# Differential attention: both queries and both keys turned in one transpose each, sums of squares and norms behind the value product's emptying

## The chip, the cores and the metric

The kernel runs on one core of a Trainium2 chip. The metric is the device time of one execution in microseconds, the median of several runs. A core has a matrix engine (PE, TensorE, with its weight loads shown as PEld), three engines for vector work (DVE or VectorE, ACT or ScalarE, POOL or GpSimd), and a queue engine (SP, SyncE) that here issues most of the DMAs. Each engine runs its own instructions in order and waits for the others by semaphores.

## The reference

The program is one decoder layer for 1024 tokens of width 1024: three branches (an mLSTM, differential attention, cross-attention into a memory), gates, projections, and an MLP. The change lies in the differential attention: 8 heads, each with two queries and two keys of width 64 and a value of width 128.

```python
def diff_attention(q, k, v, q_g, k_g, lam, subln_g, lam_init):
    q = rms_norm(q, q_g)
    k = rms_norm(k, k_g)
    ...
        s = jnp.einsum('bhcqd,bhckd->bhcqk', qblk, kt).astype(jnp.float32) * scale
        ...
        s = jnp.where(kpos[None, :] <= qpos[:, None], s, -jnp.inf)
        p = jax.nn.softmax(s, axis=-1)
        a = p[:, :, 0] - lam * p[:, :, 1]
        return jnp.einsum('bhqk,bhkv->bhqv', a.astype(vt.dtype), vt)
    ...
    o = rms_norm(o, subln_g) * (1.0 - lam_init)
```

Here `c` counts the two queries and keys of a head, and `rms_norm` divides by the root of the mean square over the 64 (or 128) elements of a head.

## The kernel before

The branch stands at about 611 to 1156 us of the span. Products are kept near float32 by splitting an operand into a high part and a low part (the rest), and multiplying the parts.

**The projection** is `d_gemm` (L1036), a generator. One step, called a piece here, is three matmuls of 128 x 384 (`mm3`, one eighth of the 1024 inputs); `fill(n)` runs n pieces. Eight pieces make a tile of 128 tokens, with 384 columns: two queries, two keys (64 each) and a value (128). Four tiles make a half head, numbered j from 0 to 15, two to a head. Tiles alternate between two PSUM banks, `mm0` and `mm1`; `other_tile` gives the bank of the tile before, once that one is emptied, and the transposes called `pr` go there. At the end of a tile `evict` empties it: ACT casts the high part of the value (`dv`), DVE subtracts to get its low part, ACT copies queries and keys into `draw`, and ACT squares them into `dscr`. A closure put into `self.after` sums the squares on DVE into `drr`; with the fourth tile two POOL instructions (`rsqrt_mean`, L140 and L141, a power) make the reciprocal roots of the half head, and the list `self.prep` of the steps that turn queries and keys is set.

**The turns.** `draw` holds each query and each key twice over, side by side (the copy has a broadcast of 2). So one transpose of a 128 x 128 piece of it gives the 64 rows of a query on partitions 0 to 63 and again on 64 to 127; a turn is four such transposes, one for each tile. For a query, ACT casts the turn into `dq` with a factor, and DVE subtracts on one half of the partitions to get the low part there; the high part stays on the other. For a key, ACT copies the turn into `dk` (the high part, on both halves) and DVE subtracts into `dkl` (the low part, both halves). The keys are scaled by `drr` before their turns, by four DVE multiplications; the queries are scaled later, in the exponential. There are four turns in a half head: query 0, query 1, key 0, key 1.

**The main loop** of `branch_d` (L1112) has 64 slots and five more to drain, eight to a head, one for each tile of queries. Slots are numbered by their place in the head (0 to 7) below. A prologue of eight steps (L1254) runs the projection of the first two half heads. In slot s stand, in this order in the code: the scores of the first query (`scores(s, 0)`: matmuls `sc`, then on DVE a mask with a maximum, shown as CUSTOM_DVE_ANT_0, and a small step, then on ACT the exponential `dpe`), `after()`, the combination of the two softmaxes of slot s - 1 (`combine`: a reciprocal, a small step and the wide `dpe` on DVE), four pieces, the value product of slot s - 2 (`po`, emptied by ACT and DVE into `doS`), the first function of the list `prep`, a piece, the scores of the second query, the transposes `tp` of the combined softmax of slot s - 1 with their emptying into `daT`, the second exponential, the remaining pieces, and the second function of `prep`. The norm of the attention's output, per half head, is cut into parts 0 to 3 (`norm`): squares, a sum with the power on POOL, a multiplication of `doS`, and a turn `tp<-doS` whose emptying is `yd`. Weights (`w<-raw`) are cast and split in between, by `ahead`.

DVE and ACT are wrapped in `InOrder` here, so both run in the order of the code. The pools give the buffers: `tp` and `po` share a ring of two banks, `sc` has two.

The lines of `evict`, before, on which much hangs:

```python
            A.copy(rw, ps[:, 0:256].rearrange("p (a d) -> p a d", a=4).unsqueeze(2).broadcast_to([P, 4, 2, 64]))
            scr = pool.tile([P, 256], F32, tag="dscr", name=self.name("dscr"))
            A.activation(scr, ps[:, 0:256], AF.Square)
```

Of the kernel before, what the change touches and what calls it, by code (L numbers as in the profile page):

```python
# [10 lines left out]
F32 = mybir.dt.float32  # L11
F32R = mybir.dt.float32r
# [5 lines left out]
P = 128  # L18
# [13 lines left out]
def f32(ap):  # L32
    return ap.bitcast(F32)
# [38 lines left out]
class Layer:  # L72
# [963 lines left out]
    def d_gemm(self, pool, kv):  # L1036
# [40 lines left out]

        def evict(ps, i, raws, vh, rr):
            v = pool.tile([P, 2, P], F32R, tag="dv", name=self.name("dv"))
            self.split2(v[:, 0], v[:, 1], ps[:, 256:384])  # L1080
            rw = pool.tile([P, 4, 2, 64], F32, tag="draw", name=self.name("draw"))
            A.copy(rw, ps[:, 0:256].rearrange("p (a d) -> p a d", a=4).unsqueeze(2).broadcast_to([P, 4, 2, 64]))
            scr = pool.tile([P, 256], F32, tag="dscr", name=self.name("dscr"))
            A.activation(scr, ps[:, 0:256], AF.Square)
            raws.append(rw)
            vh.append(v)

            def rest():
                V.tensor_reduce(rr[:, i], scr.rearrange("p (a d) -> p a d", a=4), axis=AX.X, op=ALU.add)
                if i == 3:  # L1090
                    rl = rr.rearrange("p a b -> p (a b)")
                    self.rsqrt_mean(rl, rl, 64, 16)
                    self.prep = turns(raws, rr, vh)

            self.after.append(rest)

        for j in range(16):
# [3 lines left out]
            vh, raws = [], []  # L1101
            for i in range(4):
# [6 lines left out]
                evict(ps, i, raws, vh, rr)  # L1109
                yield True  # L1110

    def branch_d(self, pool, dw):  # L1112
# [140 lines left out]

        for n in range(8):  # L1254
            fill(1)
            after()
            fill(3)
            p = self.prep.pop(0) if self.prep else None
            if p:
                p[0]()  # L1260
            fill(2)
            ahead(n)
            fill(2)
            if p:
                p[1]()
        for s in range(NS + 5):
# [4 lines left out]
            after()  # L1271
            if 1 <= s <= NS:
                combine(s - 1)
            if hh >= 1 and i == 0:
                norm(hh - 1, 1)
            fill(4)
            if 2 <= s < NS + 2:
                values(s - 2)
            if hh >= 1 and i == 1:
                norm(hh - 1, 2)  # L1280
            p = self.prep.pop(0) if self.prep else None
            if p:
                p[0]()
            fill(1)
# [24 lines left out]
            fill(2)  # L1309
            if p:  # L1310
                p[1]()
# [506 lines left out]
    def run(self):  # L1818
        tc, nc = self.tc, self.nc
        with ExitStack() as ctx:  # L1820
# [22 lines left out]
            with ExitStack() as c1:  # L1843
# [33 lines left out]
                with self.rings(("rpg", 2), ("ptm", 1), ("wpg", 14)) as (self.rp, ptm, self.wp):  # L1877
# [7 lines left out]
                    with tc.tile_pool(name="pd", bufs=2) as pd, tc.tile_pool(name="pd3", bufs=3) as pd3, tc.tile_pool(name="pdm", bufs=1) as pdm, tc.tile_pool(name="pd5", bufs=7) as pd5, tc.tile_pool(name="pdv", bufs=5) as pdv, tc.tile_pool(name="pdv2", bufs=17) as pdv2, tc.tile_pool(name="pd4", bufs=4) as pd4:  # L1885
# [6 lines left out]
                        class T4:  # L1892
                            def tile(_, shape, dt, tag, name):
                                tag = "dscr2" if tag == "gt" else tag
                                p = pd5 if tag == "draw" else pdv if tag == "drr" else pdv2 if tag == "dv" else pd4 if tag in ("dk", "dkl") else pdm if tag == "dpe1" else pd3 if tag in ("daT", "dst") else pdm if tag in ("dscr", "dscr2", "y") else pd
                                return p.tile(shape, dt, tag=tag, name=name)
# [76 lines left out]
```

## Time and profile before

| | |
|---|---|
| median of 3 runs | 2192.08 us (2191.87 to 2197.32) |
| the profiled execution | 2194.59 us, of which the span is 2192.80 |
| granted clock of PE, mean | 0.999 |
| transposes `pr` | 256, in 64 turns |
| ACT's copies `draw`, 128x512 | 64, median 0.587 us |
| DVE's multiplications `draw`, 128x256 | 64, median 0.418 us |
| DVE's sums of squares `drr` | 64, mean 0.417 us |
| POOL's power on `drr` | 16, mean 2.90 us |

The span is the time from the first to the last instruction in the record; the execution takes 1.79 us more around it. Times within the span are given from its start. A row of the timeline has the start, the duration, the engine, the line, the operation, what it writes and reads, and the shapes; in brackets stands how long the engine sat idle before it, and who ended that. A helper at L67 records all of DVE's and ACT's instructions of the branch, so they are told apart by the names of what they write and read.

### The profile page before, as it was taken

The page shows a single profiled execution, that of the slowest core. Times are in us where ns is not written, and L with a number is a line of the kernel's source. Part 1 is how long each engine was busy: PE and PEld are TensorE (multiplying, and loading weights), DVE is VectorE, ACT ScalarE, POOL GpSimd, SP SyncE. Part 2 cuts the span into 40 slices and gives each one's busy share as a digit, 9 for nine tenths or more (in the row PEclk, how much of TensorE's full clock was granted, in tenths as well). Part 3 has the DMA queues.
Part 4 walks back from the last instruction along what each step waited for, and adds up shares of the span by engine and source line. Part 5 has one row for each costly group of instructions (what it writes and reads, how often), then busy time and mean ns, then how long its engine had stood idle before and what let it go on. Part 6 is the DMA issues. An engine that isn't in the chain of part 4 may idle for free.

```text
span 2192.8 us, 30563 instructions
## 1 busy us (share of the span) xinstructions
PE 2166.7 (99%) x11254; PEld 1874.8 (85%) x11254; DVE 1385.5 (63%) x2628; ACT 969.5 (44%) x1949; POOL 534.9 (24%) x709
## 2 busy tenths in 40 slices
PE   8999999999999999999999999999999999999998
PEld 6888789888899999999888888888878888788887
DVE  6455457554138888888753233454588778876678
ACT  7543445444246666666543111223433333543331
POOL 3210000000011111111100002101566667564444
PEclk9999999999999999999999999999999999999999
DMA  7032222201311111110135344435534454744442
GB/s 252 21 117 87 88 62 79 79 14 63 116 49 35 35 31 39 39 37 25 54 120 173 116 139 130 144 111 177 191 126 159 154 198 158 268 165 158 159 158 96
DMA packets 110947, 242.38 MB, mean 111 GB/s; under 512 B 10921, under 2 KB 19406, under 8 KB 108750
## 3 DMA queue, kind: packets, MB, share of 16 engines
q1 hardware_dynamic: 108494, 227.85, 31.4%
q10 hardware_dynamic: 2304, 12.58, 1.4%
q8 instruction: 88, 1.44, 0.3%
q14 instruction: 61, 0.50, 0.1%
HBM read 173.25 MB, written 67.14 MB: 110 GB/s over the span
## 4 chain that ended last, share of the span: by engine, by line
PE 77%; DVE 12%; ACT 4%; DMA 4%; issue 2%; POOL 1%; SPq 0%; ACTq 0%; POOLq 0%; DVEq 0%
PE mm L92 46%; PE p L92 21%; PE sc L92 4%; PE tp L95 2%; PE po L92 2%; DVE sc L67 1%; ACT dpe L67 1%; DVE dpe L67 1%; DMA raw<-in_wkv 1%; DVE wo L67 1%; DVE draw L67 1%; PE pr L95 1%; DVE dst L67 1%; DVE u L67 1%; POOL wraw L67 1%
## 5 line engine op out<-in xcount | busy, mean ns | idle before, releaser
L92 PE MATMUL mm<-hT,w 128*128 128x512 f32 x1920 | 464.2, 395 | 1.6 <-ACT gt L605 1.6
L92 PE MATMUL mm<-w,hT 128*128 128x384 f32 (+3 forms) x2496 | 454.6, 329 | 0.0
L92 PEld LDWEIGHTS mm<-hT,w 128*128 128x128 f32 x1920 | 353.5, 188 | 75.5 <-ACT gt L605 2.0
L92 PEld LDWEIGHTS mm<-w,hT 128*128 128x128 f32 x2496 | 388.2, 188 | 8.8
L67 POOL TENSOR_TENSOR wraw<-wraw 128x128 f32<-128x128 f32 x496 | 321.3, 672 | 171.3 <-DMA wraw<-in_wdown 127.6
L92 PE MATMUL p<-xo,wo 128*128 128x512 f32 x1344 | 307.6, 390 | 2.2 <-ACT u L67 0.7
L92 PE MATMUL p<-xd,wo 128*128 128x512 f32 x1344 | 305.7, 389 | 0.6 <-DVE acc L67 0.5
L92 PEld LDWEIGHTS p<-xo,wo 128*128 128x128 f32 x1344 | 251.3, 188 | 57.1 <-DVE u L67 2.3
L92 PEld LDWEIGHTS p<-xd,wo 128*128 128x128 f32 x1344 | 252.0, 188 | 54.1 <-DVE acc L67 1.0
L92 PE MATMUL mm<-kt,w 128*128 128x512 f32 x1152 | 261.3, 389 | 0.0
L92 PEld LDWEIGHTS mm<-kt,w 128*128 128x128 f32 x1152 | 216.3, 188 | 44.8
L67 ACT CAST wo<-wraw 128x896 fp32r<-128x896 f32 x125 | 116.5, 944 | 258.1 <-POOL wraw L67 119.7
L67 DVE TENSOR_TENSOR wo<-wraw,wo 128x896 fp32r<-128x896 f32 x125 | 155.7, 1254 | 111.6 <-ACT wo L67 109.6
L67 ACT ACTIVATE dpe<-sc,dst,drr 128x256 f32<-128x256 f32 (+7 forms) x128 | 106.7, 833 | 62.0 <-DVE dst L67 51.9
L116 ACT CAST w<-raw 128x256 fp32r<-128x256 f32 (+2 forms) x128 | 69.0, 567 | 126.6 <-PE mm L92 99.5
L117 DVE TENSOR_TENSOR w<-raw,w 128x256 fp32r<-128x256 f32 (+2 forms) x128 | 81.5, 664 | 41.7 <-ACT w L116 41.7
L67 DVE CUSTOM_DVE_ANT_0 sc<-sc,tmask 128x256 f32<-128x256 f32 (+7 forms) x128 | 96.9, 757 | 3.6 <-PE sc L92 2.4
L140 POOL TENSOR_SCALAR hss<-hss 128x4 f32<-128x4 f32 x8 | 3.5, 442 | 378.0 <-ACT mscr L907 378.0
L92 PE MATMUL mm<-mh,w 128*128 128x512 f32 x256 | 78.9, 389 | 0.0
L106 DVE TENSOR_TENSOR w<-raw,w 128x256 fp32r<-128x256 f32 (+1 forms) x64 | 27.1, 439 | 80.0 <-ACT w L105 79.4
L67 DVE TENSOR_TENSOR w<-raw,w 128x384 fp32r<-128x384 f32 (+2 forms) x112 | 65.8, 598 | 15.8 <-ACT w L67 15.6
L92 PEld LDWEIGHTS po<-dv,daT 128*128 128x128 f32 x576 | 74.8, 189 | 0.9
(325 smaller groups left out, 2947.2 us busy)
## 6 DMA issues: line engine op xcount, KB each, us to landing
wraw<-in_wup SPq DMA_DIRECT2D x64, 256.0 KB, 3.2
r_d<-xts SPq DMA_DIRECT2D x16, 1024.0 KB, 4.2
xd<-r_d SPq DMA_DIRECT2D x16, 1024.0 KB, 5.4
wraw<-in_wdown SPq DMA_DIRECT2D x64, 256.0 KB, 4.2
raw<-in_wgate SPq DMA_DIRECT2D x48, 256.0 KB, 3.1
gates<-gt SPq DMA_DIRECT2D x48, 256.0 KB, 2.1
raw<-in_wd SPq DMA_DIRECT2D x32, 384.0 KB, 3.1
kraw<-y SPq DMA_DIRECT2D x24, 512.0 KB, 4.6
```

Source lines behind the costliest of these rows:

```text
L67: return self.tc.keep_in_program_order(f(*a, **k))
L92: self.pin(self.nc.tensor.matmul(out, l, r, start=start, stop=stop))
L95: self.pin(self.nc.tensor.transpose(out, x, self.ident))
L106: low = lambda: self.V.tensor_sub(lo, src, f32(hi))
L116: nc.scalar.copy(hi, src)
L117: nc.vector.tensor_sub(lo, src, f32(hi))
L140: g.tensor_scalar(r, ss, 1.0 / width, EPS, op0=ALU.mult, op1=ALU.add)
```

## The change

`draw` is one buffer for the four tiles of a half head, and holds each query and key once. A turn transposes the two queries at once (query 0 comes to partitions 0 to 63, query 1 to 64 to 127), a second one the two keys: two turns per half head. ACT copies the two halves of the partitions by two instructions of 64 x 512, and DVE subtracts by two. The low part of a query is written to the other half of the partitions from the one it is read from. A key's high part is copied to the other half by a DMA from SBUF to SBUF (`twice`, two per half head); its low part is kept on its own half only, in four lasting buffers (`kls`) whose other halves are set to zero once. The scaling of the keys is one multiplication. The turns stand in the list as (nothing, query turn), (scaling, key turn), (nothing, the DMAs): the first function of an entry runs behind `combine`, the second behind the value product. The list is set at the end of the fourth tile, not with the last sum of squares. `after()` comes behind the second function, parts 1 and 2 of the norm at the end of the slot, and the pieces of a slot are cut into 4, 2, 1 and 1 (before 4, 1, 1 and 2). Two pools get other sizes.

```diff
--- before.py
+++ after.py
@@ -1039,50 +1039,59 @@
         nc = self.nc
         V, A = self.V, self.A
         self.after, self.prep = [], []
-
-        def turns(raws, rr, vh):
+        kls = [pool.tile([P, 2, 512], F32R, tag=f"dkl{i}", name=f"dkl{i}") for i in range(4)]
+        for t in kls:
+            nc.gpsimd.memset(f32(t[64:128, 0]), 0.0)
+            nc.gpsimd.memset(f32(t[0:64, 1]), 0.0)
+
+        def turns(rw, rr, vh, j):
 
             qT = pool.tile([P, 2, 512], F32R, tag="dq", name=self.name("dq"))
             kd = pool.tile([P, 2, 512], F32R, tag="dk", name=self.name("dk"))
-            kl = pool.tile([P, 2, 512], F32R, tag="dkl", name=self.name("dkl"))
+            kl = kls[j % 4]
+            own = (slice(0, 64), slice(64, 128))
 
             def turn(c):
                 pt = self.other_tile()
                 for i in range(4):
-                    self.transpose(pt[:, i * P : (i + 1) * P], raws[i][:, c].rearrange("p a d -> p (a d)"))
+                    self.transpose(pt[:, i * P : (i + 1) * P], rw[:, i, 2 * c : 2 * c + 2].rearrange("p a d -> p (a d)"))
                 return pt
 
-            def q_(c):
-                lo = slice(64 - c * 64, 128 - c * 64)
-                pt = turn(c)
-                A.activation(qT[:, c], pt, AF.Copy, scale=self.gd)
-                V.scalar_tensor_tensor(
-                    out=qT[lo, c], in0=pt[lo], scalar=self.gd[lo], in1=f32(qT[lo, c]), op0=ALU.mult, op1=ALU.subtract
-                )
+            def q_():
+                pt = turn(0)
+                for c in range(2):
+                    A.activation(qT[own[c], c], pt[own[c]], AF.Copy, scale=self.gd[own[c]])
+                for c in range(2):
+                    V.scalar_tensor_tensor(
+                        out=qT[own[1 - c], c], in0=pt[own[c]], scalar=self.gd[own[c]], in1=f32(qT[own[c], c]),
+                        op0=ALU.mult, op1=ALU.subtract,
+                    )
 
             def scale():
-                for i in range(4):
-                    k_ = raws[i][:, 2:4].rearrange("p c a d -> p c (a d)")
-                    V.tensor_mul(k_, k_, rr[:, i, 2:4].unsqueeze(2).broadcast_to([P, 2, P]))
-
-            def k_(c):
-                pt = turn(2 + c)
-                A.copy(kd[:, c], pt)
-                V.tensor_sub(kl[:, c], pt, f32(kd[:, c]))
-                if c == 1:
-                    kv.append((qT, kd, kl, vh, rr))
+                k_ = rw[:, :, 2:4]
+                V.tensor_mul(k_, k_, rr[:, :, 2:4].unsqueeze(3).broadcast_to([P, 4, 2, 64]))
+
+            def k_():
+                pt = turn(1)
+                for c in range(2):
+                    A.copy(kd[own[c], c], pt[own[c]])
+                for c in range(2):
+                    V.tensor_sub(kl[own[c], c], pt[own[c]], f32(kd[own[c], c]))
+
+            def twice():
+                for c in range(2):
+                    nc.sync.dma_start(f32(kd[own[1 - c], c]), f32(kd[own[c], c]))
+                kv.append((qT, kd, kl, vh, rr))
 
             none = lambda: None
-            return [(lambda: q_(0), none), (lambda: q_(1), scale), (lambda: k_(0), none), (lambda: k_(1), none)]
-
-        def evict(ps, i, raws, vh, rr):
+            return [(none, q_), (scale, k_), (none, twice)]
+
+        def evict(ps, i, rw, vh, rr, j):
             v = pool.tile([P, 2, P], F32R, tag="dv", name=self.name("dv"))
             self.split2(v[:, 0], v[:, 1], ps[:, 256:384])
-            rw = pool.tile([P, 4, 2, 64], F32, tag="draw", name=self.name("draw"))
-            A.copy(rw, ps[:, 0:256].rearrange("p (a d) -> p a d", a=4).unsqueeze(2).broadcast_to([P, 4, 2, 64]))
+            A.copy(rw[:, i], ps[:, 0:256].rearrange("p (a d) -> p a d", a=4))
             scr = pool.tile([P, 256], F32, tag="dscr", name=self.name("dscr"))
             A.activation(scr, ps[:, 0:256], AF.Square)
-            raws.append(rw)
             vh.append(v)
 
             def rest():
@@ -1090,15 +1099,17 @@
                 if i == 3:
                     rl = rr.rearrange("p a b -> p (a b)")
                     self.rsqrt_mean(rl, rl, 64, 16)
-                    self.prep = turns(raws, rr, vh)
 
             self.after.append(rest)
+            if i == 3:
+                self.prep = turns(rw, rr, vh, j)
 
         for j in range(16):
             hd, hf = divmod(j, 2)
             w = self.dw[hd]
             rr = pool.tile([P, 4, 4], F32, tag="drr", name=self.name("drr"))
-            vh, raws = [], []
+            rw = pool.tile([P, 4, 4, 64], F32, tag="draw", name=self.name("draw"))
+            vh = []
             for i in range(4):
                 s = slice((hf * 4 + i) * P, (hf * 4 + i + 1) * P)
                 ps = self.mm_tile(384)
@@ -1106,7 +1117,7 @@
                     self.mm3(ps, (self.hT[:, k, 0, s], self.hT[:, k, 1, s]), w[k], k == 0, k == NK - 1)
                     if k < NK - 1:
                         yield True
-                evict(ps, i, raws, vh, rr)
+                evict(ps, i, rw, vh, rr, j)
                 yield True
 
     def branch_d(self, pool, dw):
@@ -1251,37 +1262,36 @@
                 A.activation(y, pt, AF.Copy, scale=self.gsub)
                 self.store_y(1, hh // 2, hh % 2, y)
 
+        self.after, self.prep = [], []
         for n in range(8):
+            p = self.prep.pop(0) if self.prep else (None, None)
             fill(1)
+            if p[0]:
+                p[0]()
+            fill(1)
+            if p[1]:
+                p[1]()
             after()
-            fill(3)
-            p = self.prep.pop(0) if self.prep else None
-            if p:
-                p[0]()
-            fill(2)
+            fill(4)
             ahead(n)
             fill(2)
-            if p:
-                p[1]()
         for s in range(NS + 5):
             hh, i = divmod(s - 2, 4)
             more = s < NS
             if more:
                 scores(s, 0)()
-            after()
+            p = self.prep.pop(0) if self.prep else (None, None)
             if 1 <= s <= NS:
                 combine(s - 1)
-            if hh >= 1 and i == 0:
-                norm(hh - 1, 1)
-            fill(4)
+            if p[0]:
+                p[0]()
+            fill(4 if s > 1 else 2)
             if 2 <= s < NS + 2:
                 values(s - 2)
-            if hh >= 1 and i == 1:
-                norm(hh - 1, 2)
-            p = self.prep.pop(0) if self.prep else None
-            if p:
-                p[0]()
-            fill(1)
+            if p[1]:
+                p[1]()
+            after()
+            fill(2 if s > 1 else 4)
             if hh >= 1 and i == 2:
                 norm(hh - 1, 3)
             if more:
@@ -1306,9 +1316,9 @@
                     exp()
                 fill(1)
                 lows()
-            fill(2)
-            if p:
-                p[1]()
+            if hh >= 1 and i < 2:
+                norm(hh - 1, 1 + i)
+            fill(1)
             if 2 <= s < NS + 2 and i == 3:
                 norm(hh, 0)
         assert self.gdone == 288 and len(kv) == 16
```

What the code's order becomes on two engines, at three places. First DVE in slot 4 of the first head, from the last small steps of the first scores over the combination of slot 3 (`dpe`) to the mask of the second scores (the ISA row with `sc`; another ISA row reads its maximum). `dst` are the small steps of the softmax, and the row of `drr` with `dscr` is a sum of squares. Before:

```order
L67 ISA dst_6865 128x1
L67 SCALAR_TENSOR_TENSOR dst_6865<-dst_6865,drr_6391 128x1
L67 TENSOR_REDUCE drr_6592<-dscr_6861 128x4
L67 RECIPROCAL dst_6790<-dst_6790 128x2
L67 SCALAR_TENSOR_TENSOR dst_6790<-dst_6790,dv 128x1
L67 SCALAR_TENSOR_TENSOR dpe_6788<-dpe_6789,dst_6790,dpe_6788 128x512
L67 SCALAR_TENSOR_TENSOR doS_6742<-po_6897,dst_6715,doS_6742 128x128
L67 SCALAR_TENSOR_TENSOR dq_6877<-pr_6906,dv,dq_6877 64x512
L67 ISA sc_6916,dst_6865<-sc_6916,tmask 128x640
L67 ISA dst_6865 128x1
L67 SCALAR_TENSOR_TENSOR dst_6865<-dst_6865,drr_6391 128x1
```

Now:

```order
L67 SCALAR_TENSOR_TENSOR dst_6846<-dst_6846,drr_6402 128x1
L67 RECIPROCAL dst_6777<-dst_6777 128x2
L67 SCALAR_TENSOR_TENSOR dst_6777<-dst_6777,dv 128x1
L67 SCALAR_TENSOR_TENSOR dpe_6775<-dpe_6776,dst_6777,dpe_6775 128x512
L67 SCALAR_TENSOR_TENSOR doS_6734<-po_6873,dst_6708,doS_6734 128x128
L67 SCALAR_TENSOR_TENSOR dq_6842<-pr_6882,dv,dq_6842 64x512 x2
L67 TENSOR_REDUCE drr_6582<-dscr_6840 128x4
L67 ISA sc_6900,dst_6846<-sc_6900,tmask 128x640
L67 ISA dst_6846 128x1
L67 SCALAR_TENSOR_TENSOR dst_6846<-dst_6846,drr_6402 128x1
```

The sum of squares went from ahead of the reciprocal to behind the query turn's subtractions, of which there are now two, and so stands between them and the mask.

Second, DVE in slot 5 of the same head, from the first mask's small step to the second mask. Before:

```order
L67 SCALAR_TENSOR_TENSOR dst_6955<-dst_6955,drr_6391 128x1
L67 TENSOR_REDUCE drr_6883<-dscr_6951 128x4
L67 RECIPROCAL dst_6865<-dst_6865 128x2
L67 SCALAR_TENSOR_TENSOR dst_6865<-dst_6865,dv 128x1
L67 SCALAR_TENSOR_TENSOR dpe_6863<-dpe_6864,dst_6865,dpe_6863 128x640
L67 SCALAR_TENSOR_TENSOR doS_6742<-po_6981,dst_6790,doS_6742 128x128
L67 SCALAR_TENSOR_TENSOR dq_6877<-pr_6992,dv,dq_6877 64x512
L67 ISA sc_7002,dst_6955<-sc_7002,tmask 128x768
```

Now:

```order
L67 SCALAR_TENSOR_TENSOR dst_6935<-dst_6935,drr_6402 128x1
L67 RECIPROCAL dst_6846<-dst_6846 128x2
L67 SCALAR_TENSOR_TENSOR dst_6846<-dst_6846,dv 128x1
L67 SCALAR_TENSOR_TENSOR dpe_6844<-dpe_6845,dst_6846,dpe_6844 128x640
L67 TENSOR_TENSOR draw_6583<-draw_6583,drr_6582 128x4x128
L67 SCALAR_TENSOR_TENSOR doS_6734<-po_6961,dst_6777,doS_6734 128x128
L67 TENSOR_TENSOR dkl_6245<-pr_6972,dk_6843 64x512 x2
L67 TENSOR_REDUCE drr_6858<-dscr_6931 128x4
L67 ISA sc_6988,dst_6935<-sc_6988,tmask 128x768
```

The multiplication of `draw`, on which the key turn waits, now stands behind `dpe`; the two `dkl` of the key turn follow in the same slot. The subtraction of query 1 is gone from here, since it stands in slot 4.

Third, PE in the prologue, from the first piece of the fifth tile on: each `mm` row is a piece, `pr` rows are turns. Before:

```order
L92 MATMUL mm_6392<-w_6085,hT 128x384 x3
L92 MATMUL mm_6392<-w_6103,hT 128x384 x3
L92 MATMUL mm_6392<-w_6123,hT 128x384 x3
L92 MATMUL mm_6392<-w_6141,hT 128x384 x3
L95 MATMUL pr_6411<-ident,draw_6277 128x128
L95 MATMUL pr_6411<-ident,draw_6313 128x128
L95 MATMUL pr_6411<-ident,draw_6351 128x128
L95 MATMUL pr_6411<-ident,draw_6387 128x128
L92 MATMUL mm_6392<-w_6159,hT 128x384 x3
L92 MATMUL mm_6392<-w_6177,hT 128x384 x3
L92 MATMUL mm_6392<-w_6192,hT 128x384 x3
L92 MATMUL mm_6392<-w_6207,hT 128x384 x3
```

Now:

```order
L92 MATMUL mm_6404<-w_6085,hT 128x384 x3
L92 MATMUL mm_6404<-w_6103,hT 128x384 x3
L95 MATMUL pr_6411<-ident,draw_6256 128x128 x4
L92 MATMUL mm_6404<-w_6123,hT 128x384 x3
L92 MATMUL mm_6404<-w_6141,hT 128x384 x3
L92 MATMUL mm_6404<-w_6159,hT 128x384 x3
L92 MATMUL mm_6404<-w_6177,hT 128x384 x3
L92 MATMUL mm_6404<-w_6192,hT 128x384 x3
L92 MATMUL mm_6404<-w_6207,hT 128x384 x3
L92 MATMUL mm_6452<-w_6085,hT 128x384 x3
L92 MATMUL mm_6452<-w_6103,hT 128x384 x3
L95 MATMUL pr_6460<-ident,draw_6256 128x128 x4
```

The query turn comes after two pieces of a tile, not four, and its four transposes read one buffer. The key turn follows one tile later, where the turn of query 1 was before.

More of the change, by code (lines that the diff above doesn't have):

```diff
@@ L1884, in run @@
                                 next(dw)
-                    with tc.tile_pool(name="pd", bufs=2) as pd, tc.tile_pool(name="pd3", bufs=3) as pd3, tc.tile_pool(name="pdm", bufs=1) as pdm, tc.tile_pool(name="pd5", bufs=7) as pd5, tc.tile_pool(name="pdv", bufs=5) as pdv, tc.tile_pool(name="pdv2", bufs=17) as pdv2, tc.tile_pool(name="pd4", bufs=4) as pd4:
+                    with tc.tile_pool(name="pd", bufs=2) as pd, tc.tile_pool(name="pd3", bufs=3) as pd3, tc.tile_pool(name="pdm", bufs=1) as pdm, tc.tile_pool(name="pd5", bufs=2) as pd5, tc.tile_pool(name="pdv", bufs=5) as pdv, tc.tile_pool(name="pdv2", bufs=17) as pdv2, tc.tile_pool(name="pd4", bufs=4) as pd4:
                         self.tmask = ptm.tile([P, D], F32, name="tmask")
@@ L1894, in tile @@
                                 tag = "dscr2" if tag == "gt" else tag
-                                p = pd5 if tag == "draw" else pdv if tag == "drr" else pdv2 if tag == "dv" else pd4 if tag in ("dk", "dkl") else pdm if tag == "dpe1" else pd3 if tag in ("daT", "dst") else pdm if tag in ("dscr", "dscr2", "y") else pd
+                                p = pd5 if tag == "draw" else pdv if tag == "drr" else pdv2 if tag == "dv" else pd4 if tag == "dk" else pdm if tag.startswith("dkl") else pdm if tag == "dpe1" else pd3 if tag in ("daT", "dst") else pdm if tag in ("dscr", "dscr2", "y") else pd
                                 return p.tile(shape, dt, tag=tag, name=name)
```

## The prediction

> **What bounds the kernel now.** I read the page's head first, then the busy time by stretches, the waits of PE, and last the timeline of one head of the differential attention, where the change lies.
>
> ```profile
> span 2192.8 us, 30563 instructions
> PE 2166.7 (99%) x11254; PEld 1874.8 (85%) x11254; DVE 1385.5 (63%) x2628; ACT 969.5 (44%) x1949; POOL 534.9 (24%) x709
> 604.00:646.00 42.00, 42.00 (x239) 40.50 (x238) 13.04 (x30) 15.60 (x37) 3.11 (x2) 1.00 0.17 51
> 820.00:880.00 60.00, 59.53 (x394) 57.70 (x394) 51.49 (x138) 41.47 (x97) 8.61 (x8) 1.00 0.12 36
> ```
>
> The last two lines are stretches: width, then busy us of PE, PEld, DVE, ACT and POOL, the granted clock, the DMA share and GB/s. In the prologue of the stage (604 to 646) and in its steady part (820 to 880) PE is full at clock 1.00, and the DMA engines are nearly idle. So a matmul that goes shortens the stage, and a wait of PE lengthens it. In the steady part DVE too is busy 51.5 of 60 us: chains that run over DVE and end at PE are the danger.
>
> **What goes.** Each of the 16 half heads loses two of its four turns (a turn is four transposes `pr`): 32 turns, of which two stood in the prologue.
>
> ```profile
> 832.24 0.42 PEld L95 LDWEIGHTS pr<-ident,draw 128*128 128x128 f32 x4
> 832.63 0.47 PEld L92 LDWEIGHTS mm<-w,hT 128*128 128x128 f32 x3
> 630.38 0.53 PEld L95 LDWEIGHTS pr<-ident,draw 128*128 128x128 f32 x4
> 630.88 4.14 PEld L92 LDWEIGHTS mm<-w,hT 128*128 128x128 f32 x24
> ```
>
> The timeline (start, duration, engine, line, operation) shows a turn between two pieces of projection: from its first weight load to the next one's 0.39 us in a steady slot, 0.50 in the prologue. The saving is 30 x 0.39 + 2 x 0.50 = 12.7 us.
>
> Some waits of PE go as well, since DVE's queue is rearranged around them: the sums of squares leave the place ahead of the combination `dpe`, and four multiplications per half head become one.
>
> ```profile
> PEld tp L95 <- DVE dpe L67: 3.7, 7, 0.5
> PEld tp L95 <- DVE doS L67: 2.7, 7, 0.4
> PE tp L95 <- DVE doS L67: 2.3, 7, 0.8
> PE tp L95 <- DVE dpe L67: 1.5, 7, 0.2
> ```
>
> These are us in total, times, and the longest, in the stage. Once per head each, the transposes `tp` wait for DVE, in slot 0 (of a head's eight) for `doS` and in slot 2 for `dpe`. The weight loads lose 6.4 us, the matmuls 3.8; I take the middle, 5.1. In slot 0 the reduction of 0.4 us ahead of `dpe` goes and `tp` comes a piece of projection later; in slot 2 the four multiplications at the end of slot 1 go. The norm's steps, put off to the end of slots 2, 3, 6 and 7, take DVE time there instead, but slots 6 and 7 lose two subtractions `dkl` and slot 6 the four multiplications. Saved in all: **17.8 us**.
>
> ACT's copies `draw` are half as wide, which shortens nothing, as the steps behind them wait for DVE. The 32 new DMAs of 128 KB (`dk` to its own other half) are issued on SP behind ACT's copies and are needed two slots, some 10 us, later: nothing for PE, and 0.12 of the DMA engines in use leaves room. If that cover went, the first scores of a half head would wait. The eight memsets run on POOL before the stage, where it is idle.
>
> **What is new on the path.** The two halves of a turn are now emptied by a pair: ACT copies both, and only then DVE subtracts both, as DVE's first subtraction waits for ACT's second copy. The reduction of the sums stands behind the pair. The k turn stands one slot after the q turn, and its transposes wait for the scaling of k. So a chain now runs from PE, in slot 4, to PE in slot 5. Before, that scaling had two slots. The rows of that place, in one head:
>
> ```profile
> 851.03 0.42 PEld L95 LDWEIGHTS pr<-ident,draw 128*128 128x128 f32 x4
> 851.73 0.69 ACT L67 ACTIVATE dq<-pr,dv 128x512 fp32r<-128x512 f32 x1
> 852.45 0.76 DVE L67 SCALAR_TENSOR_TENSOR dq<-pr,dv,dq 64x512 fp32r<-64x512 f32 x1 [0.43 <-ACT dq L67]
> 853.35 0.83 DVE L67 CUSTOM_DVE_ANT_0 sc<-sc,tmask 128x640 f32<-128x640 f32 x1
> 853.81 0.59 ACT L67 CAST daT<-tp 128x512 fp32r<-128x512 f32 x1 [0.42 <-PE tp L95]
> 854.29 0.52 ACT L67 CAST w<-raw 128x384 fp32r<-128x384 f32 x1
> 854.70 0.89 ACT L67 ACTIVATE dpe<-sc,dst,drr 128x640 f32<-128x640 f32 x1
> 855.58 0.26 ACT L67 CAST dv<-mm 128x128 fp32r<-128x128 f32 x1
> 855.87 0.29 DVE L67 TENSOR_TENSOR dv<-mm,dv 128x128 fp32r<-128x128 f32 x1 [0.28 <-ACT dv L67]
> 856.08 0.96 DVE L67 CUSTOM_DVE_ANT_0 sc<-sc,tmask 128x768 f32<-128x768 f32 x1
> 857.13 0.16 DVE L67 SCALAR_TENSOR_TENSOR dst<-dst,drr 128x1 f32<-128x1 f32 x1
> 857.21 0.41 DVE L67 TENSOR_REDUCE drr<-dscr 128x4 f32<-128x256 f32 x1
> 857.53 0.15 DVE L67 RECIPROCAL dst<-dst 128x2 f32<-128x2 f32 x1
> 857.98 0.89 DVE L67 SCALAR_TENSOR_TENSOR dpe<-dpe,dst,dpe 128x640 f32<-128x640 f32 x1
> 858.77 0.42 PEld L95 LDWEIGHTS pr<-ident,draw 128*128 128x128 f32 x4
> 860.19 0.74 DVE L67 SCALAR_TENSOR_TENSOR dq<-pr,dv,dq 64x512 fp32r<-64x512 f32 x1 [0.42 <-ACT dq L67]
> 860.85 0.95 DVE L67 CUSTOM_DVE_ANT_0 sc<-sc,tmask 128x768 f32<-128x768 f32 x1
> 845.50 0.68 DVE L67 TENSOR_TENSOR doS<-doS,dso 128x512 f32<-128x512 f32 x1
> ```
>
> PE's way between the two turns is 858.77 - 851.03 = 7.74 us, with the same work after the change. The new chain, by steps from start to start: turn to first copy 0.70; to the second copy 0.58 (ACT starts the next 0.11 before a listed end, 853.81 to 854.29); to the first subtraction 0.72; two subtractions 0.66 each (860.19 to 860.85); the reduction 0.32 (857.21 to 857.53). Sum 3.64: the mask of the slot's second scores starts at 854.67, not 853.35. From there all is in line on two full queues: to ACT's exponential 1.35, behind it the cast `dv` 0.88, DVE's `dv` 0.29, the next mask 0.21, its small step 1.05, the reciprocal 0.08 (no reduction between), `dpe` 0.45, its own 0.80 (0.89 less what DVE overlaps), the scaling, and 0.03 to PE. The scaling is one multiplication of 128 x 512; the nearest row is the `doS` multiplication, 0.68. Sum 5.82. The chain takes 9.46 us, and PE waits 1.72; seven heads make **12.0 us**. (POOL's power is in time: it needs 3.3 us after the reduction, and the scaling stands 5 us behind.) Behind the waiting turn stands all of PE's slot, so nothing wins this back.
>
> The same chain runs from slot 0 to slot 1, with smaller scores:
>
> ```profile
> 823.63 0.42 PEld L95 LDWEIGHTS pr<-ident,draw 128*128 128x128 f32 x4
> 826.45 0.30 DVE L67 CUSTOM_DVE_ANT_0 sc<-sc,tmask 128x128 f32<-128x128 f32 x1
> 829.14 0.42 DVE L67 CUSTOM_DVE_ANT_0 sc<-sc,tmask 128x256 f32<-128x256 f32 x1
> 829.65 0.16 DVE L67 SCALAR_TENSOR_TENSOR dst<-dst,drr 128x1 f32<-128x1 f32 x1
> 830.94 0.35 DVE L67 SCALAR_TENSOR_TENSOR dpe<-dpe,dst,dpe 128x128 f32<-128x128 f32 x1
> ```
>
> The second mask starts at 823.63 + 3.64 = 827.27, which is 0.82 late; so the next at 829.96, its small step 0.51 later, then 0.08, 0.45, 0.27 for the narrow `dpe` (0.35 less 0.08), 0.68 and 0.03: 831.98. PE, without the old wait of about 0.4, is there at 832.24 - 0.4 = 831.83. It waits 0.15: 7 x 0.15 = **1.0 us**, more if the chain is longer, since the slack is used up.
>
> In the prologue PE does projection alone, and there the power on POOL is in the way:
>
> ```profile
> 630.20 0.42 DVE L67 TENSOR_REDUCE drr<-dscr 128x4 f32<-128x256 f32 x1 [0.94 <-ACT dscr L67]
> 631.06 2.90 POOL L141 TENSOR_TENSOR drr<-drr,mhalf 128x16 f32<-128x16 f32 x1
> 635.01 0.53 PEld L95 LDWEIGHTS pr<-ident,draw 128*128 128x128 f32 x4
> ```
>
> A piece of projection is (635.01 - 630.88) / 8 = 0.52 us. The q turn now comes after two pieces, not four, at 629.35, and waits until the tile is emptied, about 630.0 (the reduction behind the emptying began at 630.20, and ACT's copy is now half as wide; with 630.2 it would be 0.2 more): 0.65. From 630.0 the reduction begins 3.32 later; from a reduction's start to the end of the power it is 633.96 - 630.20 = 3.76; the scaling 0.71: 637.8. PE is at the k turn at 630.0 + 0.5 + 8 x 0.52 = 634.6: a wait of 3.2. The second half head has the scores between, some 0.5: 2.7, and about 0.6 at its q turn. Sum **7.1 us**.
>
> **The sum.** -17.8 + 12.0 + 1.0 + 7.1 = +2.3 us. The profiled execution took 2194.59 (span 2192.80 and 1.79 around it) and would become 2196.9; the median of the runs shown is 2192.08, so the forecast is **2194.4**. A measurement of this kernel tells about 0.3%, 6.6 us, from no change: no change, by gains and new waits that cancel.
>
> **The rivals.**
> First, the pair runs side by side. Before, a subtraction started 0.03 us after the end of the copy it reads (852.45 behind 851.73 + 0.69), and if the first did so again, each of the 16 chains would be 0.58 shorter: 7 x 0.58 + 1.0 + 2 x 0.58 = 6.3 us, giving 2188. Against it: both halves lie in one bank, and the program puts the wait on the second copy. [...] No row of before shows two engines at once in one `pr`. Chance 0.10.
>
> Second, faster: the waits in slots 5 and 1 don't come, because a link of the chain is looser than the rows (the exponential or the cast that follows it). Then only the prologue's 7.1 stand against 17.8: 2181. For it: DVE gets lighter in every other slot. Against it: ACT went from the exponential straight to the cast (854.70 + 0.89 to 855.58). Chance 0.22.
>
> Third, slower: the scaling costs as much as what it replaces.
>
> ```profile
> 863.82 1.42 DVE L67 TENSOR_TENSOR draw<-draw,drr 128x256 f32<-128x256 f32 x4
> ```
>
> Four multiplications of 128 x 256 took 1.42; the change's single one reads strided groups of 128 against a broadcast, and its bounds are 0.68 and 1.42. It stands in all 16 chains with no slack left, so 0.74 more is 11.8 us: 2206. It decides from 0.3 us more on (16 x 0.3 = 4.8, which with the 2.3 is over 6.6). Half the elements, at 0.68, is the nearer row: `doS` has the same broadcast. Chance 0.18, with any other link that is longer by as much.
>
> **How the numbers follow.** The forecast has 0.50. Its own range is 2189 to 2199 (old waits 3.8 to 6.4, the chain 0.2 either way). Faster by over 0.3% is under 2185.5: the second rival and a little of the others, 0.25. Slower is over 2198.7: the third and a little of the forecast, 0.20. The same: 0.55. The range reaches from 2180 to 2204, to the second rival and most of the third.
>
> **What would show it.** Right: half the transposes `pr`; waits of PE at `pr` for DVE's `draw`, seven of about 1.7 us, two of about 3 near 635 to 655; no waits of `tp` for `doS` or `dpe`. The first rival: the first subtraction of `dq` ahead of the second copy's end. The second: no waits at `pr` after 660. The third: a scaling of over 1 us. Wrong altogether: waits of PE at scores for the DMAs of `dk`, or at `tp` in slots 3 and 7 for the norm.

## The result and the profile after

| | before | after |
|---|---|---|
| median | 2193.01 us (4 runs, 2191.87 to 2197.32) | 2217.89 us (4 runs, 2216.46 to 2219.71) |
| ratio | | 1.011 (95% interval 1.0093 to 1.0128) |
| span of the profiled execution | 2192.8 us | 2216.8 us |
| granted clock of PE, mean | 0.999 | 0.992 |

The change makes the kernel some 25 us slower; the forecast was 2194.4, with a range that ended at 2204. First the head of the page after, and the same stretches as before with one more (width, busy us of PE, PEld, DVE, ACT and POOL, granted clock, DMA share, GB/s):

```profile
span 2216.8 us, 30386 instructions
PE 2171.0 (98%) x11126; PEld 1874.9 (85%) x11126; DVE 1376.8 (62%) x2580; ACT 955.0 (43%) x1949; POOL 534.5 (24%) x717
604.00:646.00 42.00, 38.23 (x198) 36.15 (x197) 12.06 (x25) 13.04 (x32) 3.29 (x2) 0.92 0.20 57
760.00:820.00 60.00, 57.75 (x364) 55.51 (x363) 48.55 (x128) 37.72 (x91) 8.62 (x8) 0.97 0.15 43
820.00:880.00 60.00, 57.76 (x374) 55.67 (x373) 48.98 (x127) 38.52 (x96) 8.62 (x8) 1.00 0.16 45
```

Two things are to be seen. PE now has 2.2 us of idle time in 60, where it had 0.5. And the granted clock, 1.00 in every stretch of this stage before, is 0.92 in the prologue and 0.97 in most of the steady part, though not in all of it. PE did fewer instructions and was busy for 4 us longer.

The waits of PE in the stage (total us, times, longest) stand at the place that the prediction named:

```profile
PE pr L95 <- DVE draw L67: 22.1, 15, 3.4
PEld pr L95 <- ACT doS L67: 14.5, 7, 2.5
PEld pr L95 <- issue: 10.4, 9, 3.7
PEld tp L95 <- DVE dpe L67: 1.4, 6, 0.2
PEld tp L95 <- DVE doS L67: 0.2, 1, 0.2
```

The weight loads of the turns wait 14.5 + 10.4 = 24.9 us. The matmuls' row names what is waited for: `draw`, the scaled keys. (The second row names ACT's `doS`, but in the trace of slot 5 that ended at 813.31, the scaling at 813.70, and the load began at 813.82.) The old waits of `tp` have gone from 6.4 us to 1.6.

The timeline of slots 4 and 5 in one head, the same place that the prediction worked through:

```profile
804.03 0.62 PE L95 MATMUL pr<-ident,draw 128*128 128x128 f32 x4
804.41 1.30 PE L92 MATMUL mm<-w,hT 128*128 128x384 f32 x6
804.69 1.38 ACT L67 ACTIVATE dq<-pr,dv 64x512 fp32r<-64x512 f32 x2
806.10 1.51 DVE L67 SCALAR_TENSOR_TENSOR dq<-pr,dv,dq 64x512 fp32r<-64x512 f32 x2 [1.11 <-ACT dq L67]
807.65 0.42 DVE L67 TENSOR_REDUCE drr<-dscr 128x4 f32<-128x256 f32 x1
808.10 0.83 DVE L67 CUSTOM_DVE_ANT_0 sc<-sc,tmask 128x640 f32<-128x640 f32 x1
809.28 0.89 ACT L67 ACTIVATE dpe<-sc,dst,drr 128x640 f32<-128x640 f32 x1 [1.00 <-DVE dst L67]
810.15 0.26 ACT L67 CAST dv<-mm 128x128 fp32r<-128x128 f32 x1
810.65 0.95 DVE L67 CUSTOM_DVE_ANT_0 sc<-sc,tmask 128x768 f32<-128x768 f32 x1
812.22 0.89 DVE L67 SCALAR_TENSOR_TENSOR dpe<-dpe,dst,dpe 128x640 f32<-128x640 f32 x1
813.02 0.68 DVE L67 TENSOR_TENSOR draw<-draw,drr 128x512 f32<-128x512 f32 x1
813.85 1.09 PE L95 MATMUL pr<-ident,draw 128*128 128x128 f32 x4 [1.89 <-DVE draw L67]
814.59 2.27 PE L92 MATMUL mm<-w,hT 128*128 128x384 f32 x6
```

The chain is the one foreseen, from `pr` over the pair, the reduction, the mask, the exponential, `dv`, the next mask, `dpe` and the scaling to `pr`. It takes 9.82 us, not 9.46. Then look at the two ends: the same four transposes take 0.62 us at 804.03 and 1.09 at 813.85, the same six matmuls 1.30 and then 2.27. PE is slower behind the wait. Stretches of 2 us about this wait, and about the same wait one head later, show it (the clock is the third number from the end):

```profile
810.00:812.00 2.00, 1.97 (x15) 1.81 (x13) 1.74 (x7) 1.09 (x6) 1.41 (x1) 1.00 0.00 0
812.00:814.00 2.00, 0.15 (x1) 0.18 (x2) 1.93 (x4) 1.31 (x3) 0.00 (x0) 0.96 0.00 0
814.00:816.00 2.00, 2.00 (x8) 2.00 (x9) 0.00 (x0) 1.00 (x2) 0.00 (x0) 0.50 0.00 0
816.00:818.00 2.00, 2.00 (x12) 1.86 (x11) 1.76 (x3) 0.16 (x1) 0.00 (x0) 0.69 0.57 130
...
874.00:876.00 2.00, 0.49 (x5) 0.52 (x6) 1.62 (x3) 0.97 (x3) 0.00 (x0) 1.00 0.00 0
876.00:878.00 2.00, 2.00 (x15) 1.92 (x14) 0.61 (x1) 1.16 (x2) 0.00 (x0) 1.00 0.04 11
```

Behind the wait at 812 to 814 the granted clock is half for about 3.4 us. Behind the wait at 874 it stays full. What the half clock costs can be read from POOL's power `drr`, which is done once for each half head; here is every second one, three heads one after the other:

```profile
781.82 2.90 POOL L141 TENSOR_TENSOR drr<-drr,mhalf 128x16 f32<-128x16 f32 x1
843.47 2.90 POOL L141 TENSOR_TENSOR drr<-drr,mhalf 128x16 f32<-128x16 f32 x1
903.56 2.90 POOL L141 TENSOR_TENSOR drr<-drr,mhalf 128x16 f32<-128x16 f32 x1
```

With the half clock the distance is 61.65 us, without it 60.09: one such stretch costs 1.56 us. That half clock is the largest thing that the prediction hadn't in it.

The last piece of the loss stands behind the stage, where PE computes the gates:

```profile
PEld mm L92 <- ACT gt L605: 3.2, 2, 2.0
PE mm L92 <- ACT gt L605: 2.3, 2, 1.6
```

Before, no such waits stood there.

### The profile page after: what moved, and what is told of

Its sections match the earlier page's. It is cut to its first block, busy times and chain, and to the rows that moved or that the text cites. A ratio compares the mean times of both kernels' runs of the same rounds, so it can differ in the third digit from the quotient of the medians.

```text
span 2216.8 us, 30386 instructions
## 1 busy us (share of the span) xinstructions
PE 2171.0 (98%) x11126; PEld 1874.9 (85%) x11126; DVE 1376.8 (62%) x2580; ACT 955.0 (43%) x1949; POOL 534.5 (24%) x717
## 5 line engine op out<-in xcount | busy, mean ns | idle before, releaser
L92 PE MATMUL mm<-w,hT 128*128 128x384 f32 (+3 forms) x2496 | 461.5, 332 | 0.0
L92 PEld LDWEIGHTS mm<-w,hT 128*128 128x128 f32 x2496 | 394.5, 191 | 10.7 <-PE mm L92 1.7
L67 POOL TENSOR_TENSOR wraw<-wraw 128x128 f32<-128x128 f32 x496 | 315.3, 661 | 174.0 <-DMA wraw<-in_wdown 114.2
```

Of the source, the lines that this page charges most:

```text
L67: return self.tc.keep_in_program_order(f(*a, **k))
L92: self.pin(self.nc.tensor.matmul(out, l, r, start=start, stop=stop))
```

## The experiments

Three theories were put against each other. A: the loss is the wait at the key turn, and the slower clock behind it. B: the clock falls for another reason, or the removed turns are worth less than reckoned. C: the new places of the norm and the sums of squares cost the time. In each experiment the kernel before ran beside it; its median there was 2191.3 to 2191.9.

**The key turn one slot later.** The scaling then has a slot of its own, so that nothing on PE waits for it.

```diff
-            return [(none, q_), (scale, k_), (none, twice)]
+            return [(none, q_), (scale, none), (none, k_), (twice, none)]
```

> The key turn comes one slot later (query turn, scaling, key turn, the two DMAs: one slot each), all else as in the change. Theory A (the loss is the wait of PE at the key turn, plus a slower clock of PE behind that wait): no wait of PE for draw, granted clock 1.00 through the stage, and the saving of 32 turns (12.7) and of the old waits (5.5) shows, less 2.6 at the gates behind the stage: 2193 - 15.6 = about 2177. Theory B (the slower clock has another cause in the change than the wait): the clock stays at about 0.97 in the stage, some 12 us more, about 2189. Theory C (the new places of the norm and the sums of squares cost the time): slower than 2193.

Measured: 2190.51 us, ratio 0.9996 (0.9987 to 1.0005); clock 1.00 in all stretches of the stage; no wait for `draw`. 27 us of the change's time go by moving one turn by one slot, and the clock goes back to full with the wait, as A has it. But 2177 was expected: 13 us of the gain don't show. The waits of the stage, and the timelines of DVE and PE in slots 6 and 7, say where most of them are:

```profile
PEld tp L95 <- PE sc L92: 12.5, 14, 1.4
PE tp L95 <- DVE dpe L67: 6.8, 13, 1.0
...
810.62 0.68 DVE L67 TENSOR_REDUCE dso<-dscr 128x4 f32<-128x512 f32 x1
811.22 0.28 DVE L67 TENSOR_TENSOR dv<-mm,dv 128x128 fp32r<-128x128 f32 x1
811.42 1.22 DVE L67 CUSTOM_DVE_ANT_0 sc<-sc,tmask 128x1024 f32<-128x1024 f32 x1
...
813.26 1.15 DVE L67 SCALAR_TENSOR_TENSOR dpe<-dpe,dst,dpe 128x896 f32<-128x896 f32 x1
...
814.56 0.63 PE L95 MATMUL tp<-ident,dpe 128*128 128x128 f32 x4 [0.67 <-DVE dpe L67]
```

The norm's reduction `dso`, put off to the end of slot 6, stands ahead of `dv`, of the mask and so of `dpe`, and the transposes wait for that. So C is right for a part: a wait that the change took from slots 0 and 2 is now in slots 7 and 3.

**Work put into the wait.** This separates the wait from the clock. `pr` has its bank long before, so PE can do matmuls into it that the transposes overwrite.

```diff
             def turn(c):
                 pt = self.other_tile()
+                if c == 1:
+                    for _ in range(16 if j < 2 else 8 if j % 2 == 0 else 0):
+                        self.mm(pt[:, 0:384], self.hT[:, 0, 0, 0:P], self.hT[:, 0, 0, 0:384], start=True, stop=True)
```

> As the change, but ahead of each key turn on which PE waits long, PE does matmuls of 128x384 that nobody reads, into the bank of the turn: 16 for the first two half heads, 8 (1.4 us) for every other one from the third on. The chain that PE waits for is untouched, so the moment at which the turn starts stays. Theory A: PE is not idle long enough to lose its clock; granted clock 1.00, and about 12 us are won back by work added: 2206. Theory B: the clock falls as before, 2218 or more.

Measured: 2204.68 us, ratio 1.006 (1.0046 to 1.0073). The kernel gets 13.2 us faster by 88 matmuls that nobody needs. A stretch of it, and the place of the turn:

```profile
760.00:820.00 60.00, 59.29 (x381) 56.97 (x380) 49.93 (x131) 39.12 (x97) 8.62 (x8) 1.00 0.16 45
...
805.93 1.61 PE L92 MATMUL pr<-hT 128*128 128x384 f32 x8
807.91 0.33 PE L95 MATMUL pr<-ident,draw 128*128 128x128 f32 x1 [0.37 <-DVE draw L67]
```

PE still waits for `draw`, but only 0.4 us of it idle, and the clock is 1.00. So the half clock comes from PE's idleness, and the first half of theory B falls; what the removed turns are worth is looked at below. From the first turn to the last this trace is 11.2 us shorter than the change's (628.1 to 1082.0 against 629.4 to 1094.5), which is what the clock was worth; 1.3 us more lie ahead of the stage. Reckoned from the change's own trace it comes to about 12: six stretches at 1.56, and two in the prologue, in which 5.3 us of PE's busy time ran at half clock.

**The sum of squares ahead of the turn.** In the prologue and in the slots:

```diff
+            after()
             if p[1]:
                 p[1]()
-            after()
```

> As the change, but the sum of squares stands ahead of the turn in DVE's queue. Theory A: in the prologue the power on POOL starts 3.3 us sooner, so the two waits there of 3.6 and 3.1 become about 0.6 each (-5.5) and the slow stretch behind the first goes (-2.2); in the slots the chain is 0.3 shorter, wait 1.7 in slot 5 and 0.2 in slot 1 (-4.5): about 2206; if a wait of 1.7 no longer costs the clock, 2197. Theory B: only the waits, 2208, clock as in the change. Theory C: no gain.

Measured: 2195.65 us, ratio 1.0021 (1.0011 to 1.0031), near the second of the two numbers. The chain is 0.45 shorter, and the wait at the key turn is 1.6 us in six heads; behind none of these does the clock fall:

```profile
760.00:820.00 60.00, 58.55 (x380) 56.70 (x379) 50.66 (x132) 39.47 (x97) 8.61 (x8) 1.00 0.16 45
```

The first of the heads has a wait of 2.0 us instead, and behind that one it does.

**A longer wait, on purpose.** The kernel just told, with DVE's scaling done twice in seven half heads (the first product is not read).

```diff
                 k_ = rw[:, :, 2:4]
+                if j > 1 and j % 2 == 0:
+                    more = pool.tile([P, 4, 2, 64], F32, tag="y", name=self.name("more"))
+                    V.tensor_mul(more, k_, rr[:, :, 2:4].unsqueeze(3).broadcast_to([P, 4, 2, 64]))
```

> As e4_sums_first (a wait of 1.6 us at the key turn of slot 5, no slow clock behind it), with one more multiplication of 128x512 on DVE ahead of the scaling in the seven half heads that turn in slots 4 and 5; its product is not read. The wait becomes 2.2 to 2.3. Theory A with a threshold between 1.6 and 2.0 us: PE loses its clock behind most of these waits, and the time grows by 7 x 0.65 = 4.6 for the waits and about 1.7 a piece for five to seven slow stretches, 8 to 12: 2208 to 2212. Without the threshold (clock not a matter of the wait's length): 2200.

Measured: 2207.88 us, ratio 1.007 (1.0055 to 1.0086): 12.2 us more for 5 us of waits.

```profile
700.00:760.00 60.00, 57.83 (x367) 55.82 (x365) 49.51 (x129) 38.97 (x95) 8.59 (x8) 0.97 0.16 45
760.00:820.00 60.00, 57.82 (x375) 55.95 (x375) 50.66 (x132) 39.49 (x98) 8.63 (x8) 1.00 0.16 45
820.00:880.00 60.00, 57.81 (x368) 56.03 (x367) 50.40 (x131) 37.99 (x94) 8.63 (x8) 0.97 0.16 45
```

With waits of 2.3 us (2.7 in the first head) the clock falls again in six of the seven heads (not in the one of 760 to 820). So lengthening the wait brings the half clock back: behind waits of 1.6 us it never comes, behind those of 2.0 and more it mostly does. What sets the exceptions apart stands in the last section.

**The order alone, with the four turns of before.** Here the kernel before is edited: sums of squares behind the value product, norm parts 1 and 2 at the end of the slot, pieces 4, 2, 1 and 1.

```diff
                 scores(s, 0)()
-            after()
...
                 values(s - 2)
-            if hh >= 1 and i == 1:
-                norm(hh - 1, 2)
+            after()
...
-            fill(2)
+            if hh >= 1 and i < 2:
+                norm(hh - 1, 1 + i)
+            fill(1)
```

> The kernel before with its four turns per half head, and only the order of the change: sums of squares behind the value product, norm parts 1 and 2 at the end of the slot, pieces cut into 4, 2, 1 and 1. Theory A: the old waits of PE at tp for doS and dpe go, 5.5 us: 2187.5, clock 1.00. Theory C: slower than 2193, with new waits at tp.

Measured: 2190.06 us, ratio 0.9998 (0.9989 to 1.0007). Neither number: the old waits at `tp` go, and a new one of 0.6 us a head comes, at the turn in slot 0, which now waits for ACT's squares of a tile that is emptied later. The order gives back most of what it takes.

**The norm back in its place.** The key turn one slot later, turns after four pieces in the prologue and the first slots, and parts 1 and 2 of the norm where they stood before:

```diff
             if p[0]:
                 p[0]()
+            if hh >= 1 and i == 0:
+                norm(hh - 1, 1)
...
-            if hh >= 1 and i < 2:
-                norm(hh - 1, 1 + i)
```

In the first kernel part 2 went back behind the value product, in the second it stayed at the end of the slot.

> The key turn one slot later, and parts 1 and 2 of the norm back where they stood before the change (behind the combination, and behind the value product); in the prologue and the first two slots the turns come after four pieces, not two. Theory A, as it stands now (every us of PE in this stage hangs on what stands ahead of dpe or dv on DVE; norm part 1 at the end of slots 2 and 6 makes tp wait 0.5 and 0.9 a head, part 2 at the end of slots 3 and 7 makes pr wait 0.3): these waits go, 12 us, and 1.9 in the prologue: 2190.5 - 13 = 2177. Theory C2 (any order brings its own wait, as DVE and ACT are near full in slots 6 to 0): the old waits of 0.8 a head come back, 2183 or more.

> As e7_norms_back, but only part 1 of the norm goes back behind the combination; part 2 stays at the end of the slot. Theory A: the waits of tp go (9.8 us and 1.9 in the prologue), the wait of pr of 0.3 a head stays: 2179. Theory C2: 2183 or more.

Measured: 2188.48 (0.9983, 0.9974 to 0.9992) and 2185.72 (0.9965, 0.9952 to 0.9979). Both are faster than the kernel before, and both miss what was expected: with part 2 left at the slot's end the two edits brought 5 us, not 12. A wait of `tp` of some 0.25 us stays in slot 7 and one of `pr` of 0.3 in slot 0. In the prologue the wait only changed its place: with four pieces ahead of the turn, PE's next tile waits for the bank that the turn still holds (3.8 us in four waits, in the second kernel).

**The room that came free.** The change, with an unused tile of 6 KB a partition.

```diff
                         self.tmask = ptm.tile([P, D], F32, name="tmask")
+                        room = pdm.tile([P, 1536], F32, tag="room", name="room")
+                        nc.gpsimd.memset(room[:, 0:1], 0.0)
```

> The change as it is, with an unused tile of 6 KB a partition in the stage's pool, which takes the room that the smaller draw buffers left free. Theory A: of the loss, 2.6 us stand behind the stage, at the gates, where the loads of weights are issued in another order because that room came free; with the room taken, PE's two waits for gt at 1191 to 1200 go: 2218 - 2.6 = 2215, all waits in the stage as in the change. Rival: they come from the stage ending later, and stay: 2218.

Measured: 2212.44 us, ratio 1.0092 (1.0078 to 1.0106); the waits for `gt` behind the stage are gone from the trace. The room that the smaller `draw` buffers leave lets the loads of weights on SP come in another order: in the change five loads `raw<-in_wpc` are issued from 1160 to 1174, in among those for the gates, and with the tile they come from 1183 on, behind them. Between the two traces lie 3.3 us, fewer than the 5.5 between the medians. Of these 2.3 lie ahead of the stage, which isn't explained (the traces of the first two experiments, without the tile, begin the stage 1.3 to 2 us earlier too), and only 1.6 behind the last turn; the stage itself is 0.6 longer.

**All of it together.** As the second of the two kernels above, with three pieces ahead of the prologue's turns, two in the first two slots, and the tile of 6 KB.

```diff
-            fill(3)
+            fill(2)
             if p[1]:
                 p[1]()
             after()
-            fill(2)
+            fill(3)
...
-            fill(4)
+            fill(4 if s > 1 else 2)
...
-            fill(2)
+            fill(2 if s > 1 else 4)
```

> As e8_norm1_back, with the turns of the prologue after three pieces, those of the first two slots after two, and the unused 6 KB tile in the stage's pool. Theory A: of e8's waits go some 1.5 us in the prologue and first slots (each turn there either waits for the tile's emptying or makes the next tile wait for its own, and three pieces lie between), and 1.3 at the gates behind the stage: 2185.7 - 2.8 = about 2183; what stays is 0.8 a head at tp and pr. Rival: no change, 2186.

Measured: 2181.53 us, ratio 0.9951 (0.9939 to 0.9964), against the kernel before, some 10 us: the turns that the change saves are worth having once nobody waits for the key turn. Its steady part:

```profile
820.00:880.00 60.00, 59.74 (x388) 57.62 (x387) 52.11 (x137) 40.32 (x100) 9.12 (x10) 1.00 0.17 49
```

## Why the prediction was wrong

**What held.** PE bounds the stage; the old waits of `tp` went; the key turn waits for the scaling, seven times in slots 4 and 5 and twice in and after the prologue (at 638 and 662, where 635 to 655 was said); the first subtraction waits for ACT's second copy; the scaling took 0.68, as chosen, so the third rival's price was not paid; the DMAs of `dk` held up nothing (no wait of the stage is for them). The first rival is out, since DVE's first subtraction began at the end of the second copy (806.10 behind 806.07), and the second, since there were waits in every head. So nearly every sign that was named for being right was there, and the time still lies 23 us above the forecast: no sign had been asked of the clock.

**What failed, first and largest: the price of a wait.** The sum had a wait of PE at its own length ("PE waits 1.72; seven heads make 12.0 us"). A wait of about 2 us here costs 2 us and then 1.6 us of half clock, in six heads of seven, and more behind the wait of 3.7 in the prologue. With work in the wait in its place the time fell by 13.2 us, 11 to 12 of it by the clock. This is a step that was missing, not one with a wrong number. The trace of before shows it only once, far ahead of the stage, where from 44.24 to 47.65 us the clock is 0.50 behind 3.4 us in which PE was busy for 1.29; in the stage PE was busy for 59.53 us of 60. Nor is it a price of the wait's length alone: of 17 waits of 2.0 to 2.7 us (in the change, with the sums ahead, and with the longer wait, the prologues of the last two included) 14 brought the half clock, and one of 3.2 us did not.

**Second, the chain was too short, by 0.36.** The pair was taken to overlap, 0.58 from copy to copy and 0.66 from subtraction to subtraction. On the chip the two copies took 1.38 and the two subtractions 1.51, one behind the other, and the mask began 0.45 after the reduction, not 0.32. That made waits of 2.0 us a head (2.45 in the first) out of 1.72, and 0.5 in slot 1 out of 0.15 (832.24 - 0.4 is 831.84 there, which changes nothing). The text had said that slot 1 has no slack left. All waits at the turns together are 24.9 us, where the sum had 12.0 + 1.0 + 7.1 = 20.1.

**Third, "nothing" for what the freed room moves.** The loads on SP behind the stage were not in the sum at all, and brought waits of 2.3 to 3.2 us at the gates; with the tile in that room the trace behind the last turn is 1.6 shorter.

**Fourth, the saving was somewhat too large.** Of the 24.0 us between the two spans, 24.9 are waits at turns, about 12 the clock, some 2.6 the gates, and -5 the old waits; about -10 remain for the turns, where 12.7 were reckoned. That is a remainder; the experiment with all of it together gives an estimate of its own. By POOL's power, one head takes 59.43 us before (824.07 to 883.50) and 57.89 there (821.81 to 879.70); PE's idle time in that is 0.47 and 0.25; so the four turns that a head loses are worth 1.32 us, 0.33 a turn and 10.6 for all 32, where 0.39 a turn was reckoned.

By its own terms the sum would have come out at +2.3 + 4.8 for the waits, + 12 for the clock, + 2.6 for the gates and + 2.1 for the turns: 23.8, where the spans differ by 24.0.

## What to carry to other kernels

When a step is moved so that the bound engine waits for it, the wait's length is only the first part of its price: on PE here, a wait of 2.0 us cost 3.6 in most heads, 1.56 of it by the half clock. Where waits can't be avoided, several short ones cost no more than their length (1.6 us here, with the clock at 1.00 behind them), and in a long one even useless matmuls pay (13.2 us here). And an order that is freed of one wait has to be walked on to the next: on DVE, busy here for 49 to 52 us of 60, the norm's reduction at a slot's end made `tp` wait one slot later (6.8 us of the matmuls' waits for `dpe`), and hardly did so where it had stood before, behind the combination (0.8).

## What the runs showed that had not been expected

- PE's granted clock fell to 0.50 for about 3.4 us behind most waits of 2.0 us or more (for 6.8 behind the one of 3.7 in the prologue), and behind none of the waits of 1.6 us or less. It isn't the wait's length alone that decides: the change has the same wait of 2.0 us in six heads, and in five of them the clock falls and in one (at 874) not; behind the wait of 3.2 us before 662 it doesn't either. The traces show that the moment of the wait matters as well. In the change the half clock of the stage begins at 636.35, 690.96, 752.40, 813.84, 936.72, 998.16 and 1059.60 us, and all the distances are multiples of 3.413 us (the 54.61 from the first to the second are 16 of them, the 61.44 from the second to the third 18). Divided on that grid, the trace from 604 to 1182 us has only windows at full and windows at half clock, 161 at 1.00 and 8 at 0.50. Some of them (the first number behind the width is PE's busy time):

```profile
810.43:813.84 3.41, 1.54 (x12) 1.40 (x11) 3.29 (x9) 2.00 (x5) 0.98 (x1) 1.00 0.00 0
813.84:817.25 3.41, 3.40 (x12) 3.31 (x13) 1.17 (x3) 1.16 (x2) 0.00 (x0) 0.50 0.16 35
871.87:875.28 3.41, 1.75 (x14) 1.60 (x12) 3.11 (x10) 2.19 (x7) 1.20 (x1) 1.00 0.00 0
875.28:878.70 3.42, 3.19 (x22) 3.11 (x23) 1.64 (x4) 1.51 (x3) 0.00 (x0) 1.00 0.21 48
656.83:660.24 3.41, 2.24 (x14) 1.92 (x12) 2.94 (x12) 1.39 (x6) 2.22 (x2) 1.00 0.00 0
660.24:663.65 3.41, 1.65 (x11) 1.68 (x12) 1.25 (x3) 1.53 (x4) 0.88 (x1) 1.00 0.00 0
```

  The wait before 813.84 lies in one window and leaves PE 1.54 us of work in it; the window behind it runs at half clock. The wait at 874 reaches over an edge of the grid and leaves 1.75, and the long one before 662 lies across an edge and leaves 2.24 and 1.65: the clock stays full. In the stage of all eleven traces, each on a grid of its own, a window at full clock with at most 1.55 us of PE's busy time was followed by the half clock 23 times of 24, and none of those with 1.65 or more was. So in this kernel what counts is how much of one window a wait takes. The one exception, the window from 805.13 in the experiment with the longer wait (1.48 us busy, and the clock stayed), is open.
- 6 KB of SBUF left free changed the order of loads on SP's queue behind the stage, and the waits that came of it (2.3 to 3.2 us) are more than some of the terms that the prediction weighed.
